# A two-block network on one core: late S5 input, transfers on separate queues, and chains between layers on pairs of feature tiles

## The chip, the core and the metric

The kernel runs on one NeuronCore of a Trainium2 chip. The metric is the device time of one execution in microseconds (us), the median over several runs. The engines are TensorE (PE; PEld is its weight load), VectorE (DVE), ScalarE (ACT), GpSimd (POOL) and SyncE (SP, which only issues transfers). SPq, ACTq and POOLq are an engine's instruction queue.

## What is computed

The reference is a network on 512 tokens of 1024 features, in eight layers on one residual stream x, all in float32. The first block: a pooling mixer, a feed-forward layer with a width-3 convolution and a gated GELU (ffn0), sliding-window attention, a second such feed-forward layer (ffn1). The second block modulates each normalised input with a shift and a scale made from a conditioning vector c: an S5 state-space mixer, an MLP with a squared ReLU (mlp0), an SSD (Mamba-2) mixer, a second MLP, and a final norm. What bears on the change:

```python
# first block, per layer
h = rms_norm(x, pre_g);  f = layer(h);  x = x + rms_norm(f, post_g)
# second block, per layer; cond = silu(c)
mod = cond @ ada_w[i] + ada_b[i]            # six vectors of 1024: sh1, sc1, g1, sh2, sc2, g2
h = rms_norm(x, g) * (1 + sc1) + sh1
u = h @ s5_w_in                             # S5's input projection
```

## The kernel before, in words

x lies transposed in SBUF: eight tiles `xT[k]` of 128 features by 512 tokens. A float32 product is made of three TensorE products: weights and inputs are each split into a rounded high part and the rest (`hi`, `lo`; `wh`, `wl`), and `mm3` (L217 to L220) issues hi*wh, lo*wh, hi*wl. `wchunk` (L179) loads 512 KB of weights into one of three `ws` buffers through SP (L190), splits them on ScalarE (`wh`, L203) and VectorE (`wl`, L204). S5's input weights are split with their columns permuted.

Layers are joined by `seam` (below L780). The last product of the layer before (`tail`) runs in two halves of 256 tokens, each followed by its `chain`, which has a high priority; then comes the head of the next layer (`head(0)`, `head(1)`), its first columns, again by halves. For the layers of the first block the chain is `post_add` (L426): the root of the mean square of f is made by `Norm.rs` (L297) and spread over the partitions; then per feature tile u = f * gain * root (L434), x = x + u (L437). `staged` interleaves these per tile with further stages. The sums of squares are kept by `Norm.add` (L284): ScalarE squares a tile (L291, L294), VectorE adds it to `acc` (L295), 256 columns at a time when the span is a half. `rs` sums `acc` over the partitions with matmuls against ones (pn, L303), takes the root (sr, L305, L306), makes diagonal tiles (dg, L309) and spreads them with matmuls (pn, L312).

The next layer's input is made in one of two ways. `PreScale` (late) splits x times a gain inside the chain (h, L418, L419); the root of x is applied after the projection, when its result leaves PSUM, so the head doesn't wait for it. `PreNorm` waits for the root of x, then makes u = x * gs * root (L388), adds the shift (h, L391) and splits (h, L392). Attention and both feed-forward layers use the first, S5 and the three layers after it the second. In S5, `u_out` (L1332) moves the projected tile from PSUM (usc, L1336), stores it to DRAM and loads it in another layout (U). Then eight groups of states follow: `states` (vt, rot, U; pv, scan), `outputs` (needs the C table ct; py), `gelu` (yf, gl).

Beside the layers a background list of generators runs, a unit at a time: `s5_tables` during ffn0 (tables of S5's parameters, stored to DRAM by L664; loads of B and C, L682 to L687; the small product dd on GpSimd, L760), `s5_toeplitz` (eight groups of eight loads tz, L772, a copy th on ScalarE, L775, a store, L776), and `ada_units`, which makes `mod` by `vecmat` (L466): 12 blocks of 512 columns, eight loads `as` each through SP (L483, two buffers), eight accumulations on VectorE (aa, L486, L488), three bfloat16 parts (L496, L498), column sums (L472, `sums` L475). For the first conditioned layers it runs in ffn1, and what is left at the end of a layer's body is drained ahead of its seam. The order of instructions on each engine is set by a scheduler at build time from priorities and estimated times; on the chip each engine and each queue runs in that order.

Of the kernel before, what the change touches and what calls it, by code (L numbers as in the profile page):

```python
# [11 lines left out]
F32 = mybir.dt.float32  # L12
# [50 lines left out]
def net_kernel(ctx: ExitStack, tc: tile.TileContext, I: dict, out: bass.AP, parts=ALL):  # L63
# [40 lines left out]
    eps1 = cst.tile([P, 1], F32, name="eps1")  # L104
    V.memset(eps1, 1e-6)
    eps2 = cst.tile([P, 1], F32, name="eps2")
    V.memset(eps2, 1e-5)
    mod = cst.tile([P, 96], F32, name="mod")
    cond = cst.tile([P, KD], F32, name="cond")
    cond_set = []  # L110
# [50 lines left out]
    xT = [xp.tile([P, S], F32, name=f"x{k}") for k in range(KD)]  # L161
# [78 lines left out]
    class Held:  # L240
# [23 lines left out]
        def run(self, hf, xh, xl, evac):  # L264

            for i, (W, k0, nk, c0, apart, kw) in enumerate(self.runs):
# [3 lines left out]
                for q in range(nq):  # L270
                    for ch in self.ch[i]:
                        mm_chunk(ps[:, 256 * q:256 * q + 256], ch, q, xh, xl, nk, HALVES[hf])
                for q in range(nq):
                    evac(i, q, ps[:, 256 * q:256 * q + 256], HALVES[hf])


    class Norm:
        def __init__(self):
            self.acc = None
            self.seen = set()  # L280

        def add(self, tile_, span):
            a, b = span
            if self.acc is None:  # L284
                self.acc = tt("acc")
            dst = self.acc[:, a:b]
            if a not in self.seen:
                self.seen.add(a)
                if span == FULL:
                    self.seen.add(HALVES[1][0])  # L290
                A.activation(dst, tile_[:, a:b], AF.Square)  # L291
            else:
                sq = tt("sq")
                A.activation(sq[:, a:b], tile_[:, a:b], AF.Square)  # L294
                V.tensor_tensor(dst, dst, sq[:, a:b], ALU.add)  # L295

        def rs(self, span, eps):  # L297
# [4 lines left out]
            for j in range(nb):  # L302
                T.matmul(ps[:, j * P:(j + 1) * P], self.acc[:, a + j * P:a + (j + 1) * P], ones, start=True, stop=True)  # L303
# [57 lines left out]

    class PreNorm:
# [3 lines left out]
        def __init__(self, norm, eps, modulate):  # L366
            self.norm, self.eps, self.modulate = norm, eps, modulate
            self.h = None
            i, m, gname = modulate
            self.gs = cst.tile([P, KD], F32, tag="gs", bufs=2, name=nm("gs"))  # L370
            c = i * 48 + (m + 1) * 8
            go = voff[gname] + 8 * i
            V.scalar_tensor_tensor(self.gs, mod[:, c:c + 8], 1.0, vec[:, go:go + 8], ALU.add, ALU.mult)
# [30 lines left out]
    class PreScale(PreNorm):  # L404
# [3 lines left out]
        def __init__(self, norm, eps, gain=None):  # L408
            self.norm, self.eps, self.gain = norm, eps, gain
# [1630 lines left out]
```

## Time and profile before

| | |
|---|---|
| median of 3 runs | 2486.29 us (2485.32 to 2488.64) |
| the profiled execution | 2485.38 us, of which the profile's span is 2483.7 us |
| mean granted TensorE clock | 0.972 |
| TensorE busy | 2340.7 us, 94% of the span |
| VectorE, ScalarE, GpSimd busy | 1713.8, 1142.1, 337.9 us |

In a profile row of a time line the columns are: start in us from the span's start, duration in us, engine, line of the kernel, operation, out<-in, shapes, count, and in brackets the idle time of the engine just before it and what ended it. In a row of groups: line, engine, operation, names, shapes, count, then busy us and the mean ns of one, then the idle time before them with its main releasers. Instructions of one engine overlap by their start-up, so the step from one start to the next can be shorter than a duration. The granted clock is 1.00 at 2.4 GHz and 0.50 at 1.2 GHz.

### The profile page before, as it was taken

The page shows a single profiled execution, that of the slowest core. Times are in us where ns is not written, and L with a number is a line of the kernel's source. Part 1 is how long each engine was busy: PE and PEld are TensorE (multiplying, and loading weights), DVE is VectorE, ACT ScalarE, POOL GpSimd, SP SyncE. Part 2 cuts the span into 40 slices and gives each one's busy share as a digit, 9 for nine tenths or more (in the row PEclk, how much of TensorE's full clock was granted, in tenths as well). Part 3 has the DMA queues.
Part 4 walks back from the last instruction along what each step waited for, and adds up shares of the span by engine and source line. Part 5 has one row for each costly group of instructions (what it writes and reads, how often), then busy time and mean ns, then how long its engine had stood idle before and what let it go on. Part 6 is the DMA issues. An engine that isn't in the chain of part 4 may idle for free.

```text
span 2483.7 us, 33557 instructions
## 1 busy us (share of the span) xinstructions
PE 2340.7 (94%) x12397; PEld 1972.1 (79%) x12397; DVE 1713.8 (69%) x3069; ACT 1142.1 (46%) x2038; POOL 337.9 (14%) x345
## 2 busy tenths in 40 slices
PE   7999999788979999986899999999999999999998
PEld 7877777776778888875878887889878888888888
DVE  6896989678658778786655666666777788633333
ACT  6543535467665444344543433334555554422332
POOL 1001223201200000000110210110143331200110
PEclk9999999889989999997999999999999999999999
DMA  4224443311274555552942455543433332232222
GB/s 122 88 88 140 131 142 103 125 52 51 75 206 134 180 178 165 179 173 68 306 153 77 143 166 191 188 134 92 125 105 99 107 104 80 93 102 94 95 88 72
DMA packets 297780, 311.29 MB, mean 125 GB/s; under 512 B 53569, under 2 KB 251025, under 8 KB 296593
## 3 DMA queue, kind: packets, MB, share of 16 engines
q1 hardware_dynamic: 270033, 278.22, 36.0%
q10 hardware_dynamic: 23680, 17.31, 2.3%
q0 software_dynamic: 3904, 13.63, 1.7%
q8 instruction: 97, 1.59, 0.3%
q14 instruction: 66, 0.54, 0.1%
HBM read 284.92 MB, written 24.18 MB: 124 GB/s over the span
## 4 chain that ended last, share of the span: by engine, by line
PE 74%; DVE 12%; DMA 6%; ACT 4%; issue 3%; SPq 0%; POOL 0%; DVEq 0%; ACTq 0%; POOLq 0%
PE mm L219 22%; PE mm L218 22%; PE mm L220 22%; DMA as<-in_ada_w 3%; DVE wl L204 3%; ACT wh L203 1%; DVE aa L488 1%; PE mm L1642 1%; PE mm L1643 1%; PE mm L1644 1%; PE pb L1712 1%; PE pb L754 1%; DMA tz<-d_k 1%; ACT th L775 1%; DMA d_u<-usc 1%
## 5 line engine op out<-in xcount | busy, mean ns | idle before, releaser
L218 PE MATMUL mm<-h,wh 128*128 128x512 f32 (+1 forms) x1792 | 665.6, 374 | 22.9 <-ACT h L418 7.2
L219 PE MATMUL mm<-h,wh 128*128 128x512 f32 (+1 forms) x1792 | 666.1, 372 | 6.2 <-DVE h L392 3.3
L220 PE MATMUL mm<-h,wl 128*128 128x512 f32 (+1 forms) x1792 | 664.8, 372 | 1.7 <-DVE wl L204 1.7
L203 ACT ACTIVATE wh<-ws 128x1024 fp32r<-128x1024 f32 (+1 forms) x367 | 388.0, 1060 | 563.3 <-PE mm L219 479.6
L204 DVE TENSOR_TENSOR wl<-ws,wh 128x1024 fp32r<-128x1024 f32 (+1 forms) x367 | 466.0, 1272 | 240.7 <-ACT wh L203 234.3
L218 PEld LDWEIGHTS mm<-h,wh 128*128 128x128 f32 x1792 | 346.8, 194 | 81.0 <-issue 8.5
L219 PEld LDWEIGHTS mm<-h,wh 128*128 128x128 f32 x1792 | 347.1, 194 | 63.3 <-DVE h L392 5.4
L220 PEld LDWEIGHTS mm<-h,wl 128*128 128x128 f32 x1792 | 347.3, 194 | 56.3 <-DVE wl L204 2.5
L218 PE MATMUL mm<-hi,wh 128*128 128x512 f32 (+1 forms) x1056 | 369.5, 354 | 9.0 <-ACT wh L203 7.6
L219 PE MATMUL mm<-lo,wh 128*128 128x512 f32 (+1 forms) x1056 | 372.0, 353 | 1.7 <-DVE lo L319 1.7
L220 PE MATMUL mm<-hi,wl 128*128 128x512 f32 (+1 forms) x1056 | 370.8, 353 | 0.8 <-DVE wl L204 0.8
L218 PEld LDWEIGHTS mm<-hi,wh 128*128 128x128 f32 x1056 | 200.6, 190 | 37.3 <-ACT wh L203 8.7
L219 PEld LDWEIGHTS mm<-lo,wh 128*128 128x128 f32 x1056 | 201.4, 191 | 28.5 <-DVE lo L319 2.7
L220 PEld LDWEIGHTS mm<-hi,wl 128*128 128x128 f32 x1056 | 201.2, 191 | 26.8 <-DVE wl L204 1.0
L488 DVE SCALAR_TENSOR_TENSOR aa<-as,cond,aa 128x512 f32<-128x512 f32 x168 | 132.0, 786 | 113.8 <-DMA as<-in_ada_w 112.3
L1266 POOL TENSOR_TENSOR r<-r 128x512 f32<-128x512 f32 x64 | 88.1, 1379 | 671.1 <-ACT r L1262 488.0
L760 POOL TENSOR_TENSOR dd<-ident,s5dg 16x64 f32<-16x64 f32 x16 | 69.4, 4337 | 343.1 <-DVE kt L762 336.1
L319 DVE TENSOR_TENSOR lo<-r,hi 128x512 fp32r<-128x512 f32 x64 | 48.1, 756 | 76.5 <-ACT hi L317 76.4
L1287 DVE SCALAR_TENSOR_TENSOR x<-mm,mod,x 128x512 f32<-128x512 f32 (+1 forms) x76 | 48.9, 662 | 60.6 <-PE mm L220 60.4
L496 ACT ACTIVATE ab<-aa 128x512 bf16<-128x512 f32 x72 | 44.9, 624 | 97.0 <-DVE aa L488 61.7
L317 ACT ACTIVATE hi<-r 128x512 fp32r<-128x512 f32 x64 | 40.4, 631 | 72.3 <-POOL r L1266 72.3
L295 DVE TENSOR_TENSOR acc<-acc,sq 128x256 f32<-128x256 f32 (+1 forms) x148 | 62.0, 432 | 16.4 <-ACT sq L294 11.6
(484 smaller groups left out, 3651.2 us busy)
## 6 DMA issues: line engine op xcount, KB each, us to landing
ws<-in_mlp_w SPq DMA_DIRECT2D x124, 512.0 KB, 4.0
as<-in_ada_w SPq DMA_DIRECT2D x192, 256.0 KB, 3.1
ws<-in_ffn_w_in SPq DMA_DIRECT2D x88, 512.0 KB, 3.8
ws<-in_m_w_in SPq DMA_DIRECT2D x41, 512.0 KB, 3.7
ws<-in_ffn_w_out SPq DMA_DIRECT2D x40, 512.0 KB, 3.5
ws<-in_w_o SPq DMA_DIRECT2D x16, 512.0 KB, 3.4
ct<-d_tab SPq DMA_DIRECT2D x8, 1024.0 KB, 9.5
ws<-in_s_w_glu SPq DMA_DIRECT2D x16, 512.0 KB, 5.8
```

The source lines that it names most:

```text
L203: A.activation(h_, s_, AF.Copy)
L204: V.tensor_tensor(l_, s_, f(h_), ALU.subtract)
L218: T.matmul(ps, wh, xh, start=first, stop=False)
L219: T.matmul(ps, wh, xl, start=False, stop=False)
L220: return T.matmul(ps, wl, xh, start=False, stop=last).ins
L295: V.tensor_tensor(dst, dst, sq[:, a:b], ALU.add)
L319: return hi_, V.tensor_tensor(lo[:, ts], src, f(hi[:, ts]), ALU.subtract)
L488: V.scalar_tensor_tensor(acc, st, col(k), acc, ALU.mult, ALU.add)
L496: A.activation(parts[j], acc, AF.Copy)
L760: G.tensor_tensor(dd, ident[:16, :16].unsqueeze(1).broadcast_to([16, 4, 16]), dg[:, g4].unsqueeze(2).broadcast_to([16, 4, 16]), ALU.mult)
L1266: G.tensor_tensor(r, r, r, ALU.mult)
L1287: V.scalar_tensor_tensor(xT[n][:, ts], ps, md(i, 5, n), xT[n][:, ts], ALU.mult, ALU.add)
```

## The change

Four things. (a) S5's input uses `PreScale` with the modulation's scale as gain. The root of x is multiplied in when the projected tile leaves PSUM, and the shift enters there as a bias `s5c` = shift @ s5_w_in, which two more `vecmat` blocks compute after the 12 of the modulation. (b) x is held in pairs of tiles (`xP`), f in pairs by halves; the additions onto x, the last additions onto f and the squares run 512 wide over a pair of tiles of one half; sums of squares are kept apart for whole tiles and for each half, and `rs` adds them up on TensorE. (c) `vecmat` for the first modulation and the shift, the table stores, the B and C loads, the Toeplitz loads and S5's C tables are issued by GpSimd instead of SP. (d) Attention's f tiles leave PSUM as one 512-wide copy.

```diff
-    xT = [xp.tile([P, S], F32, name=f"x{k}") for k in range(KD)]
+    xP = [xp.tile([P, 2, S], F32, name=f"x{k}") for k in range(KD // 2)]
+    xT = [xP[k // 2][:, k % 2] for k in range(KD)]
...
     class Norm:
...
+        def add2(self, src, span):
+            sq = tt("acc" if span not in self.acc else "sq")
+            A.activation(two(sq), src, AF.Square)
+            self.gather(sq, span)
+        def gather(self, sq, span):
+            if span in self.acc:
+                V.tensor_tensor(self.acc[span], self.acc[span], sq, ALU.add)
             else:
-                sq = tt("sq")
-                A.activation(sq[:, a:b], tile_[:, a:b], AF.Square)
-                V.tensor_tensor(dst, dst, sq[:, a:b], ALU.add)
+                self.acc[span] = sq
...
-                T.matmul(ps[:, j * P:(j + 1) * P], self.acc[:, a + j * P:a + (j + 1) * P], ones, start=True, stop=True)
+                src = [self.acc[FULL][:, a + j * P:a + (j + 1) * P]] if FULL in self.acc else []
+                if span in self.acc:
+                    src += [self.acc[span][:, o + j * P:o + (j + 1) * P] for o in (0, 256)]
+                for i, t in enumerate(src):
+                    T.matmul(ps[:, j * P:(j + 1) * P], t, ones, start=i == 0, stop=i == len(src) - 1)
...
         def norm(k):
-            us[k] = tt("u")[:, ts]
-            return V.scalar_tensor_tensor(us[k], ft[k][:, ts], vc(gname, g0 + k), rs, ALU.mult, ALU.mult)
+            if k % 2 == 0:
+                us[k // 2] = tt("u")
+            o = slice(256 * (k % 2), 256 * (k % 2) + 256)
+            return V.scalar_tensor_tensor(us[k // 2][:, o], ft[k // 2][hf][:, o], vc(gname, g0 + k), rs, ALU.mult,
+                                          ALU.mult)
+        def add(k):
+            if k % 2:
+                x_ = xP[k // 2][:, :, ts]
+                return V.tensor_tensor(x_, x_, two(us[k // 2]), ALU.add)
...
-        for k in range(KD):
-            nxt.add(xT[k], span)
+        for k in range(KD // 2):
+            nxt.add2(xP[k][:, :, ts], span)
...
-    def vecmat(pool, W, ncb, col, done):
+    def vecmat(pool, W, ncb, col, done, perm=False, queue=nc.gpsimd):
...
-                nc.sync.dma_start(st, W[k * P:(k + 1) * P, cb * 512:(cb + 1) * 512])
+                queue.dma_start(st, W[k * P:(k + 1) * P, cb * 512:(cb + 1) * 512])
...
+        yield from vecmat(pool, I["ada_w_2"][i], 12, lambda k: cond[:, k:k + 1], done,
+                          queue=nc.sync if i else nc.gpsimd)
+        if i == 0 and s5_on:
+            yield from vecmat(pool, I["s5_w_in_2"][0], 2, lambda k: md(0, 0, k),
+                              lambda cb, sums: V.tensor_copy(s5c[:, 4 * cb:4 * cb + 4], sums), perm=True)
...
-            nc.sync.dma_start(dr["tab"][n][:, 512 * i:512 * i + 512], o)
+            nc.gpsimd.dma_start(dr["tab"][n][:, 512 * i:512 * i + 512], o)
...
-                nc.sync.dma_start(tz[16 * s:16 * s + 16], dr["kflat"][g8, :, j:j + P].rearrange("g h j -> h g j"))
+                nc.gpsimd.dma_start(tz[16 * s:16 * s + 16], dr["kflat"][g8, :, j:j + P].rearrange("g h j -> h g j"))
...
+        def last_down(i, ps, span):
+            o = S_["ft"][i][HALVES.index(span)]
+            V.tensor_tensor(o, o, ps, ALU.add)
+            S_["sq"].add2(two(o), span)
...
-                nc.sync.dma_start(ct[n].rearrange("p i g j -> p (i g j)"), dr["tab"][n][:, 2048:])
+                nc.gpsimd.dma_start(ct[n].rearrange("p i g j -> p (i g j)"), dr["tab"][n][:, 2048:])
...
-            a = A.activation(usc.rearrange("p (s c) -> p s c", s=8)[:, :, cs], ps.rearrange("p (c s) -> p s c", s=8),
-                             AF.Copy)
+            t = tt("us")[:, :span[1] - span[0]]
+            V.tensor_tensor(t, ps, S_["pre"].rs[:, slice(*span)], ALU.mult)
+            a = A.activation(usc.rearrange("p (s c) -> p s c", s=8)[:, :, cs], t.rearrange("p (c s) -> p s c", s=8),
+                             AF.Identity, bias=s5c[:, n:n + 1])
...
-        return Layer(lambda nxt: PreNorm(nxt, eps2, (0, 0, "norm_mix_g_2")), load, head, body_, tail_,
+        return Layer(lambda nxt: PreScale(nxt, eps2, modulate=(0, 0, "norm_mix_g_2")), load, head, body_, tail_,
```

The eight zero stores and the B and C loads of `s5_mats` move from `nc.sync` to `nc.gpsimd` in the same form as the table stores.

## Rows read from the trace of the kernel before

**Rows 1.** The page, busy time of each engine: us, share of the span, instructions.

```profile
PE 2340.7 (94%) x12397; PEld 1972.1 (79%) x12397; DVE 1713.8 (69%) x3069; ACT 1142.1 (46%) x2038; POOL 337.9 (14%) x345
```

**Rows 2.** Busy time by stretch: stretch, length, each engine's busy us, clock, DMA share, GB/s.

```profile
760.00:1065.00 305.00, 304.16 (x1434) 246.86 (x1433) 242.01 (x354) 134.74 (x177) 1.27 (x2) 1.00 0.52 167
1105.00:1175.00 70.00, 44.38 (x302) 42.24 (x302) 48.72 (x113) 28.34 (x55) 4.97 (x12) 0.76 0.28 95
```

**Rows 3.** Time line of TensorE in the seam from ffn1 to S5.

```profile
1114.16 0.60 PE L312 MATMUL pn<-dg,ones 128*128 128x128 f32 x4
...
1131.13 0.58 PE L218 MATMUL mm<-h,wh 128*128 128x256 f32 x1 [1.11 <-ACT h L391]
...
1159.50 0.58 PE L218 MATMUL mm<-h,wh 128*128 128x256 f32 x1 [1.11 <-ACT h L391]
...
1174.86 0.39 PE L218 MATMUL mm<-h,wh 128*128 128x512 f32 x1
```

**Rows 4.** Time line of TensorE in the seam from ffn0 to attention.

```profile
489.00 1.19 PE L312 MATMUL pn<-dg,ones 128*128 128x128 f32 x4 [0.97 <-DVE dg L309]
...
491.94 0.58 PE L218 MATMUL mm<-h,wh 128*128 128x256 f32 x1 [1.75 <-ACT h L418]
...
509.85 0.50 PE L218 MATMUL mm<-h,wh 128*128 128x256 f32 x2 [1.75 <-ACT h L418]
...
526.41 0.28 PE L220 MATMUL mm<-h,wl 128*128 128x256 f32 x1
```

**Rows 5.** Time line of VectorE in the seam from ffn1 to S5.

```profile
1115.52 1.88 DVE L204 TENSOR_TENSOR wl<-ws,wh 128x1024 fp32r<-128x1024 f32 x1 [0.41 <-ACT wh L203]
1117.31 0.86 DVE L434 SCALAR_TENSOR_TENSOR u<-f,vec,pn 128x256 f32<-128x256 f32 x2
...
1123.46 3.06 DVE L295 TENSOR_TENSOR acc<-acc,sq 128x256 f32<-128x256 f32 x6
```

**Rows 6.** The modulation's vector product: its accumulations as a group, two block sums in time.

```profile
L488 DVE SCALAR_TENSOR_TENSOR aa<-as,cond,aa 128x512 f32<-128x512 f32 x168 | 132.0, 786 | 113.8 <-DMA as<-in_ada_w 112.3
...
817.13 0.16 DVE L475 TENSOR_REDUCE sums<-pn 128x4 f32<-128x12 f32 x1
...
1109.20 0.15 DVE L475 TENSOR_REDUCE sums<-pn 128x4 f32<-128x12 f32 x1
```

**Rows 7.** Groups by line and shape: additions of 256 and 512 columns, partition sums.

```profile
L437 DVE TENSOR_TENSOR x<-x,u 128x256 f32<-128x256 f32 x64 | 26.5, 416 | 0.0
...
L979 DVE TENSOR_TENSOR f<-f,mm 128x512 f32<-128x512 f32 x16 | 10.5, 682 | 3.0 <-PE mm L220 3.0
...
L303 PE MATMUL pn<-ones,acc 128*128 128x128 f32 x88 | 15.7, 307 | 24.9 <-DVE acc L295 24.7
```

**Rows 8.** The end of ffn0: time line of SP, then of TensorE.

```profile
440.85 0.34 SPq L664 DMA_DIRECT2D d_tab<-ph  x1
441.99 0.37 SPq L190 DMA_DIRECT2D ws<-in_ffn_w_out  x1
...
446.91 0.39 PE L218 MATMUL mm<-hi,wh 128*128 128x256 f32 x1 [1.23 <-ACT wh L203]
```

**Rows 9.** From attention to ffn1: a stretch (columns as rows 2), time lines of ScalarE and TensorE.

```profile
700.00:720.00 20.00, 16.69 (x121) 15.93 (x120) 15.86 (x34) 16.97 (x29) 0.00 (x0) 0.91 1.04 263
...
733.74 2.03 ACT L775 ACTIVATE th<-tz 128x1024 f32<-128x1024 f32 x1 [5.50 <-DMA d_tab<-th]
...
737.11 1.19 PE L312 MATMUL pn<-dg,ones 128*128 128x128 f32 x4 [6.13 <-DVE dg L309]
```

**Rows 10.** S5's groups: a wait of TensorE for a C table, SP's waits before C tables.

```profile
1223.66 0.70 PE L1382 MATMUL py<-U,ct 128*128 128x128 f32 x2 [4.14 <-DMA ct<-d_tab]
...
SPq L1329 <- PE py L1383: 22.6, 5, 7.7
```

**Rows 11.** GpSimd by line and shape: a load that it issues, and a small product.

```profile
L1321 POOL DMA_DIRECT2D vt<-d_tab x16 | 8.8, 551 | 448.6 <-DVE aa L488 337.8 <-DVE acc L295 96.6 <-PE mm L219 7.8
...
L760 POOL TENSOR_TENSOR dd<-ident,s5dg 16x64 f32<-16x64 f32 x16 | 69.4, 4337 | 343.1 <-DVE kt L762 336.1 <-DMA s5dg<-in_s_d 6.9
```

More of the change, by code (lines that the diff above doesn't have):

```diff
@@ L109, in net_kernel @@
     cond = cst.tile([P, KD], F32, name="cond")
+    s5c = cst.tile([P, KD], F32, name="s5c")
+    s5_on = "s5" in parts
     cond_set = []
@@ L262, in load_run, with run @@
             self.ch[i] += self.ap[i]
-        def run(self, hf, xh, xl, evac):
+        def run(self, hf, xh, xl, evac, banks=False):
             for i, (W, k0, nk, c0, apart, kw) in enumerate(self.runs):
@@ L360, in behind, with modulated @@
             yield
+    def modulated(i, m, gname):
+        gs = cst.tile([P, KD], F32, tag="gs", bufs=2, name=nm("gs"))
+        c = i * 48 + (m + 1) * 8
+        go = voff[gname] + 8 * i
+        V.scalar_tensor_tensor(gs, mod[:, c:c + 8], 1.0, vec[:, go:go + 8], ALU.add, ALU.mult)
+        return gs
     class PreNorm:
@@ L406, in net_kernel, with __init__ @@
         late = True
-        def __init__(self, norm, eps, gain=None):
-            self.norm, self.eps, self.gain = norm, eps, gain
+        def __init__(self, norm, eps, gain=None, modulate=None):
+            self.norm, self.eps = norm, eps
+            if modulate is not None:
+                gs = modulated(*modulate)
+                self.gain = lambda k: gs[:, k:k + 1]
+            else:
+                self.gain = lambda k: 1.0 if gain is None else vc(gain[0], gain[1] + k)
             self.h = [(ht(), ht()) for _ in range(KD)]
@@ L415, in parts @@
             ts = slice(*span)
-            g = [1.0 if self.gain is None else vc(self.gain[0], self.gain[1] + k) for k in range(KD)]
+            g = [self.gain(k) for k in range(KD)]
             hi, lo = ([h[i][:, ts] for h in self.h] for i in range(2))
@@ L970, in head, with down @@
             hd.run(hf, pre.hi, pre.lo, evac)
-        def down(n, ps, span, first, last):
-            ts = slice(*span)
-            ft = S_["ft"]
-            if first:
-                ft.append(at("f"))
-                A.activation(ft[n], ps, AF.Copy)
-            else:
-                V.tensor_tensor(ft[n][:, ts], ft[n][:, ts], ps, ALU.add)
-                if last:
-                    S_["sq"].add(ft[n], span)
+        def down(n, ps, first):
+            if first and n % 2 == 0:
+                S_["ft"].append([at("f") for _ in range(2)])
+            for hf in range(2):
+                o = S_["ft"][n // 2][hf][:, 256 * (n % 2):256 * (n % 2) + 256]
+                p_ = ps[:, slice(*HALVES[hf])]
+                if first:
+                    A.activation(o, p_, AF.Copy)
+                else:
+                    V.tensor_tensor(o, o, p_, ALU.add)
+        def last_down(i, ps, span):
+            o = S_["ft"][i][HALVES.index(span)]
+            V.tensor_tensor(o, o, ps, ALU.add)
+            S_["sq"].add2(two(o), span)
         def body_():
@@ L1020, in tail_ @@
                 warm_sqrt(S_["split"].ins)
-            tl.run(hf, S_["ah"], S_["al"], lambda i, q, ps, span: down(2 * i + q, ps, span, False, True))
+            tl.run(hf, S_["ah"], S_["al"], last_down, banks=True)
         return Layer(lambda nxt: PreScale(nxt, eps1, ("ffn_pre_g", 8 * l)), hd.load, head, body_, tail_,
```

90 lines of the change are left out of this document (50 added, 40 removed).

## The prediction

> **What bounds the kernel now.** I read four views in this order. First the busy times of the engines: TensorE is busy for 2340.7 us of a span of 2483.7 us [rows 1]. So at most some 140 us are plainly idle, and the question is where they lie. Second, the busy times by stretch: in the body of the second feed-forward layer (760 to 1065 us) TensorE is busy for 304 of 305 us at the full clock, so no edit that only frees a queue or VectorE can shorten it; in the seam from that layer to S5 (1105 to 1175) it is busy for 44.4 of 70 us, and the granted clock averages 0.76, which mixes the two levels of 1.2 and 2.4 GHz [rows 2]. Third, the time lines of TensorE and VectorE in that seam. After the reciprocal root of the sum of squares of f is spread (1114.16), VectorE updates x, then six dependent additions for the new sum of squares take 3.06 us, a second root is taken, and only then the first matmul of S5's input starts, at 1131.13; the second half starts at 1159.50, and the first 512-wide matmul behind the head at 1174.86 [rows 3, 5]. Fourth, the same stretch of a seam whose next layer takes its input without waiting for that second root (feed-forward to attention): spread at 489.00, first head matmul at 491.94, second half at 509.85, last head matmul at 526.41 [rows 4]. Both heads are 96 matmuls of 256 columns per half (two weight groups, two tiles, eight k, three products), so the second seam is a measurement of what the first becomes.
>
> **Part 1, late input of S5.** Removed: the wait for the second root ahead of the head. From spread to the end of the head it is 1174.86 - 1114.16 = 60.7 us now, and 526.41 + 0.28 - 489.00 = 37.7 us in the late seam [rows 3, 4]: 23 us less. In S5's seam VectorE still splits a permuted weight until 1117.4, so its first update comes at 1117.31, some 2 us later than the spread allows [rows 5]; that wait stays: 21 us less. What moves: the 16 normalisations of VectorE go, and 12 multiplications by the root come at the head's evacuation, 8 of 256 and 4 of 512 columns, at 0.42 and 0.68 us each (the nearest two-operand rows) [rows 7] 6.1 us, against 16 x 0.43 = 6.9 us by the update of the same form (two in 0.86 us) [rows 5]; I count that as even.
>
> Added: the product of the shift with the input weights. It is 16 more loads and accumulations of 512 columns at 0.79 us [rows 6], 12.6 us, and four permuted subtractions, for which the permuted weight split is the nearest row (1.88 us for 1024 columns [rows 5], 0.94 each), 3.8 us: 16.4 us of VectorE. They stand at the end of the background queue, and that queue is already late: its last block sums at 1109.20, inside the seam [rows 6]. VectorE is busy for 48.7 of 70 us there [rows 2]; a seam 20 us shorter leaves almost no room. Lower bound 0 (they fill holes while loads are awaited), upper bound all 16.4 on the path; I take 8, the middle, since the bias is needed only at the evacuation, yet VectorE runs in order. Part 1 is then 21 - 8 = **13 us less**, between 5 and 23.
>
> **Part 2, chains on pairs.** Each of the 16 sums of squares of the four late chains, and the halves of the others, become 3 additions of 512 instead of 7 of 256 columns. Six dependent ones took 3.06 us, 0.51 each [rows 5]; scaled by 0.68/0.42 [rows 7] the new ones are 0.83 each, 2.5 us: about 0.5 us less per sum, 11 us for 22 sums. The additions onto x or f give 4 x (2 x 0.416 - 0.682) = 0.6 us per half, 12 halves: 7 us. Against that, the partition sum on TensorE now takes two matmul groups per 128 columns, three where whole and half tiles meet: 88 records now [rows 7], 104 more by the diff (16 late sums and 2 of the modulated ones with 4 more each, 4 of the modulated ones with 8), and a group of four takes 0.60 us [rows 3], 0.15 each: 15.6 us. Each pair's first split also waits for the second update. About half of either side lies on a path. I take **0**, between -12 and +12.
>
> **Part 3, queues.** 272 issues go to POOL: 16 table stores, 8 zero stores, 64 loads of B and C, 64 of the Toeplitz loads, 96 modulation loads, the 16 new ones, and 8 C tables. At 0.55 us [rows 11] that is 150 us of an engine busy for 338 us of the span [rows 1]. The gain is what stood behind them on SP. At the end of the first feed-forward layer SP holds a table store until VectorE has made it, at 440.85; the weight load behind it goes out at 441.99, and TensorE is idle for 1.23 us before 446.91, waiting for the split of a weight [rows 8]; I take 2 us for it and smaller stops of the kind, between 0 and 4. From attention to the feed-forward layer the 64 Toeplitz loads (one line, eight times eight) go out on SP between the weights; ScalarE waits 5.50 us for the store of one Toeplitz copy, and the next root on ScalarE queues behind it: TensorE idles 6.13 us [rows 9]. I take 5 us, between +5 and -13. In S5's groups TensorE waits 4.14 us for one C table [rows 10]; I take 2, between +4 and -4. Nothing in the second feed-forward body, which has no hole to fill [rows 2]. Together **9 us less**.
>
> A row speaks against the middle term: in 700 to 720 the 16 DMA engines are at a share of 1.04 [rows 9], so the loads compete after they are issued as well. The Trainium skill, "DMA: Bandwidth & Descriptors", section "Issuing engines are not separate DMA queues", goes further: issuing from several engines saves only issue time, since all run on the same engines. By it part 3 would be 0 and the sum 9 us higher. The wait on SP in rows 8 is one in order, before any transfer, which that sentence doesn't cover.
>
> What queues behind the moved waits: behind a modulation load that waits for VectorE now stand the V tables of S5 (the vt loads); behind a C table that waits for the outputs of TensorE now stand POOL's dec, xs and gl of the next group; behind a table store the next B and C loads and dd.
>
> **The sum.** The profiled execution took 2485.38 us, 0.9 below the median of the three runs (2486.29). 2485.4 - 13 - 0 - 9 = **2463 us**.
>
> **Rivals.**
> *Queues change nothing* (transfers compete anyway): for it the DMA share of 1.04, against it rows 8. 2485.4 - 13 = 2472.
> *The vector product decides the seam*: background blocks were paced at (1109.20 - 817.13) / 11 = 26.6 us each [rows 6]; two more at that pace end at 1162, where the head could have ended near 1174.86 - 21 = 1154. The evacuations wait for the bias, and the next projection for their PSUM banks, so that nothing of part 1 is left: 2485.4 - 9 = 2476. For it: the blocks already reach into the seam. Against: the loads no longer share a queue.
> *C tables on POOL hold up the S5 groups*: SP's waits for them are 22.6 us in five [rows 10]; if they all stand before dec and xs on the path, 2463 + 22.6 = 2486, no change. Against it: only two buffers are involved, and POOL waits anyway for VectorE.
> *Slower: POOL can't keep up.* Beside VectorE, POOL's 16 x 64 products take 4.34 us, and 0.55 us is the rule for its loads [rows 11]. If the 112 issues of modulation and shift took 4.34 us, they would need 486 us from about 790 on (one block ahead of the sum at 817.13), to 1276; S5's evacuation, which now follows the second half's start at 1159.50, would wait some 115 us: near 2485 + 115 - 9 = 2591. It decides as soon as an issue costs more than (1160 - 790) / 112 = 3.3 us. The mean of the 16 vt issues, four of them in the busy S5 seam, is against it. The Trainium skill, "SBUF — State Buffer", section "SBUF: two separate sides", warns of exactly this: descriptors of loads issued from GpSimd are starved while VectorE is in a two-port mode. By it the time would be this rival's.
>
> **How the numbers follow.** Chances: forecast 0.50, queues nothing 0.16, vector product 0.16, C tables 0.08, POOL starved 0.06, other mishaps of order 0.04. A measurement of this kernel can tell about 0.2%, 5 us. Faster than 2481: all of the first, most of the next two: 0.77; within 5 us: 0.12; slower: 0.11. The range takes in a part 1 at -23 with queues of -18 at the low end (2444) and the C tables, with 2 us over, at the high end: 2444 to 2488.
>
> **What would show it.** Right: in the S5 seam the first head matmul some 5 us behind the spread of the root, the second half 20 us behind it, no long gap of TensorE between the two halves; SP's weight loads at the end of the first feed-forward layer without standing behind a table store; POOL issues of as near 0.55 us. Wrong: the usc evacuation waiting for s5c; a POOL issue above 1 us; ACT th still ahead of a root; the pn groups of eight costing more than the acc additions give back.

## The result, and the profile after

The kernel after takes 2516.74 us (median of 4 runs, 2516.1 to 2519.0) against 2485.81 for the kernel before on the same chip: ratio 1.0126, interval 1.0109 to 1.0144. It is 31 us slower; 23 us less were forecast, and the time lies outside the range. First the busy times of the kernel after, then the two stretches of [rows 2] in it (stretch, length, busy us of PE, PEld, DVE, ACT, POOL, clock, DMA share, GB/s):

```profile
PE 2349.0 (93%) x12525; PEld 1980.3 (79%) x12525; DVE 1709.6 (68%) x2973; ACT 1147.3 (46%) x1990; POOL 478.4 (19%) x617
...
760.00:1065.00 305.00, 304.34 (x1435) 247.40 (x1434) 242.36 (x359) 133.69 (x184) 47.39 (x88) 1.00 0.52 167
1105.00:1175.00 70.00, 27.61 (x182) 25.70 (x182) 41.44 (x77) 22.93 (x38) 9.12 (x17) 0.64 0.32 113
```

The body of the second feed-forward layer is unchanged. In the seam to S5 TensorE is busy for 27.6 of 70 us instead of 44.4, and the clock falls from 0.76 to 0.64. To see where time goes elsewhere I compare when the same matmul starts: each kernel issues 3328 matmuls of the form lo*wh in the same order. First column: its start in the kernel before; then how much later (+) or earlier (-) it starts in the profiled execution of each other kernel. The letters stand for the experiments below, which each change one thing or a few.

```
before   after    b      e      f      a      i      j      n      m     where
  85.2   +11.9  +11.1   +6.3   +5.8  +11.6   +7.3   +6.4   +7.0   -1.7   ffn0, body
 404.1   +11.8  +10.8   +5.6   +5.4  +11.7   +6.8   +5.8   +6.3   -2.3   ffn0, late
 532.4   +14.2  +11.1   +3.6   +8.6  +11.9   +5.6   +4.7   +3.8   -2.2   attention, body
 630.1   +11.2   +7.3   +0.2   +7.5   +8.3   +2.0   +1.0   +0.4   -1.7   attention, body
 652.1    +4.4   +0.6   -6.6   +0.7   +1.5   -4.8   -5.7   -6.4   -3.4   attention, late
 801.8    -4.6   -9.2   -7.6   -8.1   -7.8  -13.6  -15.1  -15.4   -2.7   ffn1, body
1025.5    -4.0   -9.0   -3.0   -8.4   -7.0  -11.9  -12.1  -14.5   +0.8   ffn1, late
1101.5    -7.2  -12.6   -5.5  -12.3   -7.7  -10.8  -18.3  -21.4   -2.1   ffn1, last product
1160.1   +10.0  -15.7   -8.9  -12.2  -27.3  -30.0  -27.5  -46.7   -6.7   S5 head, second half
1174.2   +18.8  -17.0  -10.0  -13.5  -18.8  -21.7  -27.9  -40.5   -8.1   S5, behind the head
1300.7   +27.6  -11.9  -11.3   -7.8   -9.6  -12.6  -27.5  -35.6   -8.9   S5, behind the groups
2483.7   +31.3   -9.6  -10.0   -7.7   -6.3   -9.2  -20.5  -32.8   -8.9   end of the span
```

Each column is one execution: that of b lies 6.5 us under the median of its runs, that of m 5.1 under, that of i 4.9 over. A difference of a few us between two columns can be chance. For the kernel after the column reads: 12 us are lost by 85 us, 19 gained between 532 and 802, 17 lost from the last product to the second half of S5's head, 9 behind that head, 9 in S5's groups.

**The seam to S5.** TensorE's time line in the kernel after, then ScalarE's, VectorE's and GpSimd's in the same stretch:

```profile
1118.56 0.27 PE L520 MATMUL pn<-one,ab 128*128 128x1 bf16 x4 [12.03 <-ACT ab L548]
...
1137.97 0.27 PE L520 MATMUL pn<-one,ab 128*128 128x1 bf16 x4 [14.87 <-ACT ab L548]
...
1143.92 2.08 PE L332 MATMUL pn<-ones,acc 128*128 128x128 f32 x8 [0.26 <-DVE sums L523]
1146.96 1.20 PE L341 MATMUL pn<-dg,ones 128*128 128x128 f32 x4 [0.96 <-DVE dg L338]
1150.66 0.80 PE L225 MATMUL mm<-h,wh 128*128 128x256 f32 x2 [2.50 <-ACT h L456]
...
1169.50 0.80 PE L225 MATMUL mm<-h,wh 128*128 128x256 f32 x2 [2.50 <-ACT h L456]
...
1136.86 1.06 ACT L548 ACTIVATE ab<-aa 128x512 bf16<-128x512 f32 x1 [14.08 <-DVE aa L536]
1137.82 0.61 ACT L313 ACTIVATE acc<-f 128x512 f32<-128x512 f32 x1
1138.34 1.65 ACT L313 ACTIVATE sq<-f 128x512 f32<-128x512 f32 x3
...
1109.40 0.68 DVE L1041 TENSOR_TENSOR f<-f,mm 128x512 f32<-128x512 f32 x1
...
1123.21 0.16 DVE L523 TENSOR_REDUCE sums<-pn 128x4 f32<-128x12 f32 x1
...
1134.48 0.75 DVE L536 SCALAR_TENSOR_TENSOR aa<-as,mod,aa 128x512 f32<-128x512 f32 x1 [1.66 <-DMA as<-in_s_w_in]
...
1143.70 0.17 DVE L523 TENSOR_REDUCE sums<-pn 128x4 f32<-128x12 f32 x1 [1.51 <-PE pn L520]
...
1128.82 0.54 POOL L531 DMA_DIRECT2D as<-in_s_w_in  x1 [0.68 <-DVE aa L536]
```

The fourth addition of f's first half runs at 1109.4, but ScalarE squares f only at 1137.8: in its queue the squares of f stand behind four part copies (ab) of the two shift blocks, and those wait for loads and accumulations. The two blocks end at 1123.2 and 1143.7, 20.5 us apart; the partition sum of f (L332) runs 0.2 us behind the second. In the meantime TensorE stands idle ahead of the blocks' column sums. The group of all column sums in the whole kernel, before and after, shows it in its last numbers:

```profile
L472 PE MATMUL pn<-one,ab 128*128 128x1 bf16 x288 | 16.1, 166 | 2.5 <-ACT ab L496 2.5
```

```profile
L520 PE MATMUL pn<-one,ab 128*128 128x1 bf16 x312 | 17.6, 166 | 36.8 <-ACT ab L548 36.6
```

From there on the seam is what was forecast: first head matmul 3.7 us behind the spread, second half 18.8 us behind the first, no long stop between.

**The start.** GpSimd, VectorE and TensorE in the first 16 us of the kernel after:

```profile
2.20 0.90 POOL L738 DMA_DIRECT2D bs<-in_s_b_re  x1
...
7.04 0.54 POOL L743 DMA_DIRECT2D cs<-in_s_c_re  x1
...
8.48 0.35 DVE L907 TENSOR_TENSOR band<-band,ident 128x128 f32<-128x128 f32 x1 [7.38 <-POOL band L886]
...
15.05 0.77 PE L938 MATMUL mm<-band,xr 128*128 128x128 f32 x2 [5.32 <-DVE xr L923]
```

GpSimd issues eight loads of B and C, 2.2 to 7.6 us, ahead of most of the pooling layer's band masks, which it also makes; VectorE's first use of a mask comes at 8.48 instead of 3.30, and TensorE's first pooling product at 15.05 instead of 8.04.

**Attention to ffn1.** The Toeplitz copy th still stands ahead of a root on ScalarE, and TensorE stops for 3.72 us where it stopped for 6.13 [rows 9]:

```profile
748.20 2.05 ACT L831 ACTIVATE th<-tz 128x1024 f32<-128x1024 f32 x1
750.03 0.23 ACT L334 ACTIVATE sr<-pn,eps 128x2 f32<-128x2 f32 x1
...
750.93 0.68 PE L341 MATMUL pn<-dg,ones 128*128 128x128 f32 x4 [3.72 <-DVE dg L338]
```

### The profile page after: what moved, and what is told of

Read it like the earlier page. It is cut to its first block, busy times and chain, and to the rows that moved or that the text cites. A ratio compares the mean times of both kernels' runs of the same rounds, so it can differ in the third digit from the quotient of the medians.

```text
span 2515.0 us, 33743 instructions
## 1 busy us (share of the span) xinstructions
PE 2349.0 (93%) x12525; PEld 1980.3 (79%) x12525; DVE 1709.6 (68%) x2973; ACT 1147.3 (46%) x1990; POOL 478.4 (19%) x617
## 4 chain that ended last, share of the span: by engine, by line
PE 72%; DVE 11%; DMA 7%; issue 5%; ACT 4%; POOL 1%; SPq 0%; ACTq 0%; DVEq 0%; POOLq 0%
PE mm L225 21%; PE mm L226 21%; PE mm L227 21%; DMA as<-in_ada_w 4%; DVE wl L211 2%; ACT wh L210 1%; PE pn L332 1%; DVE aa L536 1%; DMA as<-in_s_w_in 1%; DMA tz<-d_k 1%; PE mm L1707 1%; PE mm L1708 1%; PE mm L1709 1%; PE pb L1777 1%; PE pb L810 1%
## 5 line engine op out<-in xcount | busy, mean ns | idle before, releaser
L548 ACT ACTIVATE ab<-aa 128x512 bf16<-128x512 f32 x78 | 51.4, 659 | 130.5 <-DVE aa L536 87.3
L531 POOL DMA_DIRECT2D as<-in_ada_w x96 | 51.7, 539 | 295.7 <-DVE aa L534 121.9
L816 POOL TENSOR_TENSOR dd<-ident,s5dg 16x64 f32<-16x64 f32 x16 | 59.4, 3713 | 88.6 <-DVE kt L818 82.2
```

What stands on the lines that cost most here:

```text
L531: queue.dma_start(st, W[k * P:(k + 1) * P, cb * 512:(cb + 1) * 512])
L548: A.activation(pv[j], av, AF.Copy)
L816: G.tensor_tensor(dd, ident[:16, :16].unsqueeze(1).broadcast_to([16, 4, 16]), dg[:, g4].unsqueeze(2).broadcast_to([16, 4, 16]), ALU.mult)
```

## The experiments

All times are medians, all ratios are to the kernel before on the same chip, with 95% intervals; the letters are those of the table above. The kernel before took 2484.2 to 2485.5 us (median) beside these runs. A ratio rests on all runs and not on the two medians: in m it stands for 5 us, the medians for 3.

| run | us | ratio |
|---|---|---|
| a: after, four background units at a step | 2480.8 | 0.9979 (0.9970 to 0.9989) |
| b: after without (a), the late input | 2482.3 | 0.9988 (0.9977 to 0.9999) |
| c: after, column sums in a PSUM bank of their own | 2510.9 | 1.0105 (1.0088 to 1.0122) |
| d: after, B and C loads back on SP | 2508.7 | 1.0096 (1.0081 to 1.0111) |
| e: pairs and single copy alone | 2478.1 | 0.9976 (0.9963 to 0.9989) |
| f: queues alone | 2477.9 | 0.9977 (0.9966 to 0.9988) |
| g: a and d | 2474.2 | 0.9959 (0.9944 to 0.9974) |
| h: a, C tables back on SP | 2479.0 | 0.9972 (0.9961 to 0.9983) |
| i: a, d and h together | 2471.3 | 0.9943 (0.9926 to 0.9960) |
| j: i with the normalised input | **2464.0** | **0.9915 (0.9901 to 0.9930)** |
| k: i, weights split behind the second root | 2478.5 | 0.9968 (0.9955 to 0.9980) |
| l: i, additions onto x tile by tile | 2475.2 | 0.9953 (0.9936 to 0.9970) |
| m: before, four background units at a step | 2481.6 | 0.9979 (0.9964 to 0.9993) |
| n: i, shift left out | 2454.9 | 0.9872 (0.9856 to 0.9889) |

### What holds up the S5 seam (a, b, c)

```diff
-            layer = ffn_layer(1, ((0, 8), (8, 16), (16, 22)))
+            layer = ffn_layer(1, ((0, 8), (8, 16), (16, 22)), rate=4)
```

> Edit: the second feed-forward layer lets the background run four units at a step of its body in place of three, nothing else. Theory 'drained work': the two shift blocks (sums at 1123.2 and 1143.7 us) don't fit into the body, are drained ahead of the seam, and ScalarE and VectorE take them before the squares of f. Then both fit, the last sums come before 1106, TensorE's stops of 12.0 and 14.9 us at 1106 and 1123 go, and the time falls by 25 to 40 us, to 2477-2492. Rival 'slow loads on GpSimd': the loads keep their pace of some 2 us each whatever the rate, the last sums come after 1120, and the time stays above 2500.

Measured 2480.8: 36 us back, and the last sums at 1103.0, as 'drained work' said. The loads did not keep a pace of their own, so 'slow loads on GpSimd' falls. TensorE behind the last product, then VectorE and ScalarE, in this run:

```profile
1113.47 0.80 PE L225 MATMUL mm<-h,wh 128*128 128x256 f32 x2 [5.00 <-ACT h L456]
...
1132.31 0.50 PE L225 MATMUL mm<-h,wh 128*128 128x256 f32 x2 [2.50 <-ACT h L456]
...
1151.37 0.97 PE L341 MATMUL pn<-dg,ones 128*128 128x128 f32 x4 [2.54 <-DVE dg L338]
1154.74 0.80 PE L225 MATMUL mm<-h,wh 128*128 128x512 f32 x1 [2.40 <-DVE us L1400]
...
1102.99 0.17 DVE L523 TENSOR_REDUCE sums<-pn 128x4 f32<-128x12 f32 x1
...
1147.06 3.76 DVE L211 TENSOR_TENSOR wl<-ws,wh 128x1024 fp32r<-128x1024 f32 x2 [0.22 <-ACT wh L210]
...
1151.33 0.42 DVE L1400 TENSOR_TENSOR us<-mm,rsx 128x256 f32<-128x256 f32 x1
...
1144.76 0.36 ACT L462 ACTIVATE rsx<-pn 128x256 f32<-128x256 f32 x1
1145.02 3.89 ACT L210 ACTIVATE wh<-ws 128x1024 fp32r<-128x1024 f32 x2
1148.82 0.24 ACT L334 ACTIVATE sr<-pn,eps 128x2 f32<-128x2 f32 x1
...
1152.98 0.37 ACT L462 ACTIVATE rsx<-pn 128x256 f32<-128x256 f32 x1
```

From the last product to the head's second half 19.6 us are gained (-7.7 to -27.3 in the table), near the 21 forecast. But 8.5 go again right behind the head. The two weight groups times two halves hold all four `mm` banks, so the next projection needs a tile to leave PSUM (1154.74). Two things come late. The second half's root (sr) stands behind two weight splits on ScalarE and two on VectorE, and its spread (1151.37) stands ahead of the projection on TensorE. And VectorE's first multiplication (us, 1151.33) stands behind the same splits, though the first half's root was there since 1145.1 (rsx): that tile leaves before the second root is copied (rsx, 1152.98). So it is the order of splits, root and tiles in the queues, and not the second root alone.

By the kernel's code the modulation makes 51 units of background work, with the shift 60. The body of ffn1 takes 48 at three units a step and 58 at four. So the kernel before drains the last three units, the kernel after twelve, among them both shift blocks, and run a only two: the split and the column sum of the last block.

```diff
-        return Layer(lambda nxt: PreScale(nxt, eps2, modulate=(0, 0, "norm_mix_g_2")), load, head, body_, tail_,
+        return Layer(lambda nxt: PreNorm(nxt, eps2, (0, 0, "norm_mix_g_2")), load, head, body_, tail_,
...
-        if i == 0 and s5_on:
-            yield from vecmat(pool, I["s5_w_in_2"][0], 2, lambda k: md(0, 0, k),
...
-            V.tensor_tensor(t, ps, S_["pre"].rs[:, slice(*span)], ALU.mult)
```

> Edit: part (a) undone (normalised S5 input, no shift product), pairs and queues kept. If the whole loss in the S5 seam belongs to (a): the time is the one that the kernel after had gained at the end of the second feed-forward body, 7 us below before: 2474-2484. If the pairs or the queues also cost in the seam: above 2490.

Measured 2482.3, inside the first range: the whole loss of the kernel after against the kernel before belongs to (a), 34 us. Pairs and queues together are worth 3 us.

```diff
-            ps = psn.tile([P, 512], F32, tag="n", name=nm("pn"))
+            ps = pp.tile([P, 512], F32, tag="n", name=nm("pn"))
...
-        work.gens.append(ada_units(opened("adp"), i))
+        work.gens.append(ada_units(opened("adp"), i, opened("adps", space=PSUM)))
```

> Edit: the column sums of the modulation and of the shift go to a PSUM bank of their own instead of the one that the norms of the seam use. Theory 'drained work' (order on ScalarE and VectorE): the squares of f still stand behind the blocks, no change, 2512-2522. Rival 'one PSUM bank': the root of f was waiting for the bank only; it starts near 1112 and the time falls by 20 to 30 us, to 2487-2497.

Measured 2510.9: 6 us, between the two ranges and 1 us from that of 'drained work'. In its trace the squares of f still start at 1137.9, behind the same four part copies, and the partition sum of f comes 2.5 us earlier than in the kernel after (1143.92), no longer behind the second block's sums:

```profile
1141.41 2.08 PE L332 MATMUL pn<-ones,acc 128*128 128x128 f32 x8
```

The order on the engines is the larger cause; the shared bank is a small one.

### The start, the pairs and the queues (d, e, f)

```diff
-                nc.gpsimd.dma_start(bs[:64, e], u[g8].rearrange("g p h -> p g h"))
+                nc.sync.dma_start(bs[:64, e], u[g8].rearrange("g p h -> p g h"))
...
-                nc.gpsimd.dma_start(cs[:, e, 1], v[g8].rearrange("g h p -> (g h) p"))
+                nc.sync.dma_start(cs[:, e, 1], v[g8].rearrange("g h p -> (g h) p"))
```

> Edit: the 64 loads of B and C go back from GpSimd to SP. The kernel after is 12 us late at 80 us. Theory 'masks behind loads': GpSimd issues eight of these loads for 5 us ahead of the band masks at the start; then the first pooling matmul comes near 8.5 instead of 15.1 us and the time falls by 4 to 8 us, to 2509-2513. Rival 'pairs': the 12 us come from the longer waits for the second tile of a pair in the first seam, and the time stays within 2 us of 2517.

Measured 2508.7, 8 us back, 0.3 us beyond the range of 'masks behind loads' and far from that of 'pairs'; the first pooling product, at 15.05 in the kernel after, comes at 7.65, and VectorE's first use of a mask at 3.31:

```profile
7.65 0.66 PE L938 MATMUL mm<-band,xr 128*128 128x128 f32 x2
...
3.31 0.35 DVE L907 TENSOR_TENSOR band<-band,ident 128x128 f32<-128x128 f32 x1 [2.21 <-POOL band L886]
```

By the same count of matmuls, 7.0 of the 11.9 us at 85 us stay.

```diff
-            nc.gpsimd.dma_start(dr["tab"][n][:, 512 * i:512 * i + 512], o)
+            nc.sync.dma_start(dr["tab"][n][:, 512 * i:512 * i + 512], o)
...
-                nc.gpsimd.dma_start(tz[16 * s:16 * s + 16], dr["kflat"][g8, :, j:j + P].rearrange("g h j -> h g j"))
+                nc.sync.dma_start(tz[16 * s:16 * s + 16], dr["kflat"][g8, :, j:j + P].rearrange("g h j -> h g j"))
...
-                          queue=nc.sync if i else nc.gpsimd)
+                          queue=nc.sync)
```

This one also undoes (a) as in b, the B and C loads as in d, and moves the zero stores and the C tables back.

> Edit: the kernel after with (a) undone and every transfer back on SP: the pairs and attention's one copy alone. The prediction counted them as 0 (-12 to +12). In the run with B and C back on SP 7 us were still lost at 80 us. Theory 'pairs lose in the first seam and give it back in the others': 2480-2490. Rival 'pairs cost wherever a chain waits for the second tile': first seam +7, and 1 to 2 us in each of the other late seams, 2492-2500.

Measured 2478.1, 6 us faster than before and 2 below the first range. The table has 6.3 us lost by 85 us (the rest of the start's 12), 11.2 gained between 532 and 802, and 3.4 gained in S5's seam. The pairs lose in the first seam and win around attention. Why there is not shown: 6.8 of the 11.2 are gained between 630 and 652, where the kernel before waits 2.54 us (643.74) for one of ScalarE's two copies of f, but run f, which keeps both copies, gains the same 6.8 there.

```diff
-                nc.sync.dma_start(tz[16 * s:16 * s + 16], dr["kflat"][g8, :, j:j + P].rearrange("g h j -> h g j"))
+                nc.gpsimd.dma_start(tz[16 * s:16 * s + 16], dr["kflat"][g8, :, j:j + P].rearrange("g h j -> h g j"))
...
-                nc.sync.dma_start(ct[n].rearrange("p i g j -> p (i g j)"), dr["tab"][n][:, 2048:])
+                nc.gpsimd.dma_start(ct[n].rearrange("p i g j -> p (i g j)"), dr["tab"][n][:, 2048:])
```

The kernel before with these and the other transfers of (c) moved.

> Edit: the kernel before with the transfers moved to GpSimd and nothing else. From the kernel after: 5 us lost at the start (loads ahead of the masks), 24 us gained from attention's body to the next seam, 6 us given back in that seam. If these belong to the queues: 2467-2477. Rival 'the attention gain belongs to the pairs or to the single copy of f': 2488-2495.

Measured 2477.9, 6 us faster, 1 us above the first range: +5.8 at the start, -16.7 between 532 and 802, +5.7 in S5's groups. Both e and f win in attention, and together (b) they win 20.3 there, not 11.2 + 16.7 = 27.9: the 6.8 (b: 6.7) between 630 and 652 come once. Their losses at the start add up (6.3 + 5.8, measured 11.1). From 652 to 802 f gains another 8.8; its stop of TensorE before the second spread is 1.73 us instead of 6.13 [rows 9]:

```profile
749.06 0.68 PE L312 MATMUL pn<-dg,ones 128*128 128x128 f32 x4 [1.73 <-DVE dg L309]
```

### Repairs together (g, h, i)

```diff
+            layer = ffn_layer(1, ((0, 8), (8, 16), (16, 22)), rate=4)
...
+                nc.sync.dma_start(bs[:64, e], u[g8].rearrange("g p h -> p g h"))
...
+                nc.sync.dma_start(ct[n].rearrange("p i g j -> p (i g j)"), dr["tab"][n][:, 2048:])
```

g has the first two, h the first and the third, i all three.

> Edit: the kernel after with four background units at a step and the B and C loads back on SP. If the two repairs are independent: 2480.8 - 8.0 = 2473, 2469-2477. Rival 'what is gained at the start is lost later at a weight load behind these on SP': 2478-2483.

> Edit: the kernel after with four background units at a step and S5's C tables back on SP. There the seam gained 20 us, but of that 8 were lost behind the head and 9 in the first groups. Theory 'C tables on GpSimd stand before dec, xs and gl': the groups get back 4 to 9 us, 2472-2477. Rival 'the groups lose to something else (clock, order of the outputs)': 2479-2484.

> Edit: the kernel after with three repairs: four background units at a step, B and C loads and C tables back on SP. If the third adds to the first two as it did alone (2 us): 2474.2 - 2 = 2472, 2468-2475. If it only moved a wait: 2473-2478.

g 2474.2 and i 2471.3 came as the sum said. h at 2479.0 is 2 us below a, at the edge of the rival's range, and i 3 below g: the intervals overlap, so the C tables' order is worth a few us at most. One wait goes with them: of TensorE in run a, in the last groups,

```profile
1238.90 0.77 PE L1448 MATMUL py<-xs,ct 128*128 128x128 f32 x2 [3.95 <-DVE xs L1439]
```

is absent in h, whose longest stop between 1225 and 1260 is 1.69 us. The same stop, 3.95 to 4.08 us, stands in the trace of the kernel after and of each run whose C tables GpSimd issues (a, b, c, d, f, g), and in none whose C tables SP issues.

### What the late input is worth (j, k, l, m, n)

Run j is i with the diff of b. In j nothing is drained (last sums at 1041.4). In i only the split and the column sum of the last shift block run after the start of ffn1's last product at 1090.7; its sums come at 1100.3.

> Edit: the same three repairs, but with the normalised S5 input of before and no shift product: against the run before it in this call, the worth of the late input alone, with nothing drained in either. Theory 'most of the seam's 21 us stays': this one is 8 to 15 us slower, 2480-2487. Rival 'what the late input gains between root and head it gives back behind the head (evacuations waiting for the second root, all PSUM banks held) and in the first groups': within 4 us, 2468-2476.

Measured 2464.0: nothing is left of the late input, and it seems to cost 7 us (the intervals of i and j still overlap a little, 0.9926 and 0.9930). Neither range held it. The table gives the places (i less j, in one execution each, 11.3 in all): the end of the body +7.3, where the two shift blocks run; the seam -10.0; behind the head +8.7; the groups +8.7; later -3.6. The evacuation of S5's tiles in j, in i and in n (minimum, median and maximum ns of one):

```profile
L1396 ACT ACTIVATE usc<-mm x12: 365/399/598, 1134.4 to 1170.6; 128x256 f32<-128x256 f32 x8, 128x512 f32<-128x512 f32 x4
```

```profile
L1401 ACT ACTIVATE usc<-us,s5c x12: 743/778/1337, 1149.5 to 1179.0; 128x256 f32<-128x256 f32 x8, 128x512 f32<-128x512 f32 x4
```

```profile
L1397 DVE TENSOR_TENSOR usc<-mm,rsx x12: 602/636/1122, 1131.8 to 1158.4; 128x256 f32<-128x256 f32 x8, 128x512 f32<-128x512 f32 x4
```

ScalarE's part alone takes 0.78 us instead of 0.40, with VectorE's product ahead of it.

```diff
+                later = []
+                chs = list(chunks(win, 0, KD, j * P, perm=True, later=later))
+                with behind([S_["pre"].last]):
+                    for split_ in later:
+                        split_()
```

> Edit: on top of the three repairs, the splits of the weights of the projection that follows S5's head are put behind the second root of x. With four units at a step the second root (ScalarE sr at 1148.8) stood behind two weight splits of 1.9 us, and TensorE stopped twice 2.5 us behind the head. Theory 'the root is late because of these splits': the stops shrink and the time falls 2 to 5 us against the first run of this call. Rival 'the weights are as late as the root': the stop moves to the split, no gain or 1 to 3 us slower.

Measured 2478.5, no faster than i (7 us above it, more than the rival's 3, with intervals that overlap a little). The root comes first, and TensorE waits for the split instead, as the rival said; ScalarE's evacuations of the head's tiles now stand behind the splits:

```profile
1145.27 0.50 PE L225 MATMUL mm<-h,wh 128*128 128x512 f32 x1 [2.60 <-ACT wh L210]
...
1148.85 3.40 ACT L1401 ACTIVATE usc<-us,s5c 128x256 f32<-128x256 f32 x5
```

By the same count of matmuls k loses 4.8 us behind the head, where i loses 8.3, and 17.4 in the groups, where i loses 9.1. So the new order helps behind the head by 3.5 us, and more than that is lost later.

```diff
-            if k % 2:
-                x_ = xP[k // 2][:, :, ts]
-                return V.tensor_tensor(x_, x_, two(us[k // 2]), ALU.add)
+            o = slice(256 * (k % 2), 256 * (k % 2) + 256)
+            return V.tensor_tensor(xT[k][:, ts], xT[k][:, ts], us[k // 2][:, o], ALU.add)
```

> Edit: on top of the three repairs, the additions onto x run tile by tile again (256 columns); squares, sums and f stay in pairs. In the late seams the first head matmul now comes 2.50 us behind the spread of the root, 1.84 before. Theory 'the second tile is waited for': 0.65 us in each of eight chain halves and less of the low clock behind them, 3 to 8 us faster than the first run of this call. Rival 'VectorE's shorter time pays for it': within 2 us, or slower.

Measured 2475.2 with an interval that overlaps that of i: no gain, inconclusive beyond that. The cause of the pairs' 6 us in the first seam stays open. In the groups l loses 2.5 us, though its S5 layer is that of i.

Run m is the kernel before with the diff of a.

> Edit: the kernel before with four background units at a step of the second feed-forward body, nothing else. The prediction took the 60.7 us from spread to the end of S5's head as the wait for the second root. Theory 'part of it was the modulation's own drained block (sums at 1109.20)': with nothing drained the seam shortens by 6 to 12 us and the time is 2474-2480. Rival 'the block was hidden behind the tail': 2483-2488.

Measured 2481.6, 5 us faster than before by the ratio, the interval's ends 2 to 9 us: between the two ranges. In the table its seam (1101.5 to 1160.1) shortens by 4.6 us. So some 5 us of the seam of before were its own drained work, and not the wait for the second root.

```diff
-            t = tt("us")[:, :span[1] - span[0]]
-            V.tensor_tensor(t, ps, S_["pre"].rs[:, slice(*span)], ALU.mult)
-            a = A.activation(usc.rearrange("p (s c) -> p s c", s=8)[:, :, cs], t.rearrange("p (c s) -> p s c", s=8),
-                             AF.Identity, bias=s5c[:, n:n + 1])
+            ph = lambda t: t.rearrange("p (c s) -> p s c", s=8)
+            a = V.tensor_tensor(usc.rearrange("p (s c) -> p s c", s=8)[:, :, cs], ph(ps),
+                                ph(S_["pre"].rs[:, slice(*span)]), ALU.mult)
```

> Edit: the kernel with three repairs and the late input, but the shift is left out of S5's input: no shift product, and the evacuation is one VectorE product from PSUM into the permuted tile in place of product and biased ScalarE copy. Against the one with the normalised input (2464.0): theory 'the shift's work is what eats the late input's gain' (blocks in the body, two-step evacuation): 2450-2461. Rival 'the late root itself eats it (nothing leaves PSUM until the second root is spread, all banks held)': 2462-2470.

n also leaves out the two shift blocks in `ada_units`. Measured 2454.9: 9 us below j, 16 below i, as 'the shift's work' said. By the table 8.0 of what n gains on i lie at the end of the body (-6.9, i +1.1; j, which has no blocks either, -6.2). TensorE's first head matmul and the first product behind the head in n, and the same two in i:

```profile
1093.80 0.50 PE L225 MATMUL mm<-h,wh 128*128 128x256 f32 x2 [0.19 <-ACT h L456]
...
1133.03 0.79 PE L225 MATMUL mm<-h,wh 128*128 128x512 f32 x1 [0.48 <-DVE usc L1397]
```

```profile
1110.74 0.80 PE L225 MATMUL mm<-h,wh 128*128 128x256 f32 x2 [5.00 <-ACT h L456]
...
1151.89 0.80 PE L225 MATMUL mm<-h,wh 128*128 128x512 f32 x1 [2.03 <-DVE us L1400]
```

The 5.0 us before the head are gone (stops of 1.8 and 1.0 follow in it), and of the two stops behind it the second, for the evacuation, is 0.5 us. n still loses 6.2 us behind the head (-46.7 to -40.5). Here too VectorE multiplies the first half's tiles before the second root is copied, and only after three weight splits:

```profile
1131.83 2.20 DVE L1397 TENSOR_TENSOR usc<-mm,rsx 128x256 f32<-128x256 f32 x4
...
1132.62 0.38 ACT L462 ACTIVATE rsx<-pn 128x256 f32<-128x256 f32 x1
```

How much of the 6.2 us is the late root and how much the place of the splits is not separated.

## Why the prediction was wrong

**The step that failed is the price of the shift product**, "16.4 us of VectorE", with 16.4 as the upper bound and 8 taken. It counted VectorE's busy time. What stood on the path was the elapsed time of the blocks: 20.5 us each, since eight loads go through two buffers and each accumulation waits for its own, and the splits go back and forth between ScalarE and VectorE. Two blocks are 41 us; TensorE idled 36.8 us ahead of column sums (2.5 before), and run a gave 36 back. The lower bound hoped that "they fill holes while loads are awaited". But the chain couldn't run while the blocks awaited their loads, because its squares stood behind them in ScalarE's queue. The rival "the vector product decides the seam" had the right place and the right point (blocks ending after the head could), and a wrong price: it let the chain run beside the blocks and charged only the bias, 8 us. With b as the measure, part 1 cost 34 us where 13 less stood, and parts 2 and 3 together gained 3 where 9 stood.

**"21 us less" for the late seam** was right where it looked (19.6 in run a) and incomplete. It compared spread to end of head in two seams, and left out what follows the head, where the tiles' multiplications and the second root now meet the next projection's weight splits: 8.5 us. It also took a seam of before that contained drained work of its own, worth about 5 us (run m). Against a seam without any, the late input gains not 21 us there but 10 with the shift (i less j) and 16 without it (n less j). The "even" exchange of normalisations for evacuations was priced on VectorE alone; ScalarE's part went from 0.40 to 0.78 us, behind VectorE's product. By i less j, part 1 sums to +7 us with its blocks in the body, where -13 stood.

**Part 2, 0 between -12 and +12**, measured -6 (run e), inside its bounds, but not by its sum. The sum set six additions of before against three, while its own count was seven; by that count a sum of squares saves 1.1 us, not 0.5. The 104 added partition sums are there as counted (192 records against 88) and cost TensorE 12.6 us more, where 15.6 stood; its wait for the additions ahead of them falls from 24.9 us [rows 7] to 16.8 in run e:

```profile
L332 PE MATMUL pn<-ones,acc 128*128 128x128 f32 x192 | 28.3, 290 | 16.8 <-DVE acc L318 16.7
```

More than the whole gain came around attention, 11.2 us, for a reason that no run shows.

**Part 3, -9**, measured -6 (run f), near by luck, with each term off. The end of the first feed-forward layer: 2 us less forecast, 2.7 more measured (+5.4 at 404, +8.1 at 493 us). Attention to ffn1: 5 forecast, 8.8 measured (652 to 802), and 6.8 more inside attention that the prediction did not look for. C tables: 2 less forecast, 5.7 more measured in the groups, of which putting the tables back returned 2 to 3 by the medians of h and i. So the rival "C tables on POOL hold up the S5 groups" had the right place, with a stop of some 4 us, not 22.6. And the start, 5.8 more, had no term: the prediction named what queues behind moved *waits*, but not behind the moved loads themselves, the band masks. That two parts of a change can win the same time once (20.3 instead of 27.9 us in attention) was not considered either.

**"Slower: POOL can't keep up"** had the sign and the wrong mechanism. GpSimd's loads of the modulation and of the shift in the kernel after (busy us, mean ns of one, idle before them):

```profile
L531 POOL DMA_DIRECT2D as<-in_ada_w x96 | 51.7, 539 | 295.7 <-DVE aa L534 121.9 <-DVE aa L536 114.6 <-DVE sums L523 29.9
L531 POOL DMA_DIRECT2D as<-in_s_w_in x16 | 8.6, 538 | 34.3 <-DVE aa L536 20.9 <-DVE sums L523 5.4 <-DVE aa L534 5.3
```

0.54 us each beside a VectorE at 242 of 305 us, far from the 3.3 us that this rival needed. The Trainium skill, "SBUF — State Buffer", section "SBUF: two separate sides", warns that descriptors can't be written while VectorE is in a two-port mode; these rows don't show it, nor whether VectorE's accumulations ran in such a mode. GpSimd is busy for 140.5 us more than in [rows 1], as counted (150).

**Left open:** why S5's groups lose 9 us with the late input (i, a), 5 without the shift (n) and 2.5 in l. The evacuation and a lower clock (0.83 in i's 1200 to 1220) go with it, but no run separates them. Why both e and f gain 6.8 us between 630 and 652, and what the pairs lose in the first seam, is open too.

## What to carry to other kernels

A background task that misses its last slot is drained ahead of the next layer and can cost its elapsed time, loads and hand-overs included, not its busy time: count its units against the slots of the body before adding to it. An input that takes its scale late moves work from ahead of the head to the evacuation; price the evacuation on each engine, and look at what stands ahead of it in each queue. A moved transfer delays what its new queue does next, so look at the first use of that engine in each layer, the start of the kernel included; here the version that keeps pairs and most queues, leaves the late input out and drains nothing beats both kernels (2464.0 us).

## What the runs showed of the hardware

A permuting ScalarE evacuation of 256 and 512 columns took 0.40 us (median) as a copy from PSUM and 0.78 us with a bias from SBUF; which of source and function matters was not tried. A GpSimd issue of the B loads took 0.69 to 0.75 us on average, against 0.53 to 0.57 for the loads of C, the Toeplitz blocks and the modulation, all in the kernel after:

```profile
L828 POOL DMA_DIRECT2D tz<-d_k x64 | 33.6, 532 | 37.0 <-ACT th L831 22.2 <-issue 8.6 <-ACT h L456 4.5
L738 POOL DMA_DIRECT2D bs<-in_s_b_re x8 | 6.0, 746 | 4.8 <-DVE tb L768 4.7
```
